# A fourth seven-product quad per gate-and-up column, and half of the other quads' low parts made by an accumulating DMA

## The chip, the cores and the metric

The kernel runs on one core of one Trainium2 chip. The metric is the device time of one execution in microseconds, the median of several runs.

## The reference

A two-layer trunk for 256 tokens of width 2048, all in float32. Both layers end in a SwiGLU block, and this is where the change is:

```python
D_MODEL = 2048; SEQ = 256; D_FF = 5632

def swiglu(h, w_gate, w_up, w_down):
    return (jax.nn.silu(h @ w_gate) * (h @ w_up)) @ w_down

def reference(x, ...):
    for layer in range(2):
        h = rmsnorm(x, g_mix[layer])
        ...
        x = x + mix
        x = x + swiglu(rmsnorm(x, g_ffn[layer]), w_gate[layer], w_up[layer], w_down[layer])
    return rmsnorm(x, g_final)
```

Layer 0 mixes tokens with a gated unit and mean pools, layer 1 with latent attention; both mixers are left as they are.

## The kernel before

**Products in two parts.** TensorE takes float32 operands in a form (float32r, F32R) with fewer bits. So every operand is split: a high part, the value rounded to that form, and a low part, the rest. One product of a 128x128 block of tokens with a 128x512 block of weights is three matmuls (`token_product`, L207 to L209): high x high, high x low, low x high. The weights come as raw tiles of 128x2048 (1 MB, three buffers, issued by SP). ScalarE copies 1024 columns to the high part `wh` (L101), then VectorE subtracts it from the raw tile to give the low part `wl` (L102). There are six tiles of either kind, used in turn, so a new part waits until TensorE is through with the one six parts earlier.

**The feed-forward block** (`feed_forward`, L554). The 5632 hidden columns are worked off in three parts of 4, 4 and 3 columns of 512 (`PARTS`). A column is computed from eight quads j = 0 to 7. A quad is 256 rows of the weights: two row blocks of gate and two of up, four blocks of 128x512 in one raw tile, against 2 x 2 blocks of 128 tokens x 128 features. The four sums c11, c12 (gate and up for the first 128 tokens), c21, c22 stand in PSUM. An eight-quad does the eight block products directly (L579 to L582). A seven-quad does a Strassen-Winograd step with seven (L586 to L594): it needs sums and differences of the four weight blocks, made by VectorE in `quad_seven` (L512), and forms of the tokens' blocks (`forms`, tile `ckv`), made once per layer in `put_pair` (L266). `SEVEN` names the seven-quads, 3, 5 and 7. So a column is 5 x 8 + 3 x 7 = 61 products, 183 matmuls.

The split of a seven-quad is the tile `sums` (t1, t3, t2, t4) and four blocks. In order: VectorE makes t1 and t3 in one subtraction (L519), the first pair of blocks (b22, b21) is split, t2 (L521) and t4 (L522) are made, then the second pair (t2, t4), b11 alone (512 columns) and the third pair (t1, t3) are split. An eight-quad is two splits of 1024 columns.

After a column, ScalarE copies PSUM sums to SBUF, VectorE adds the seven-quads' partial sums in eight additions (L604 to L611), ScalarE applies SiLU and VectorE multiplies; eight transposes on TensorE turn the result, and it is split to `hid`. The transposes wait in a list, `pending`, and are let out after quads 1 and 2 (L595) of the next column. After each part the down projection follows (`into_trunk`), 16 or 12 raw tiles in two plain splits each.

**What sets the order.** `chunks_of` (L532) is a generator of split tiles: it issues loads and splits so that three tiles are ready or under way (`AHEAD` = 2) when one is asked for. The order of instructions on each engine is then set at build time by a scheduler, and each engine works its own queue in order.

Two lines carry most of it:

```python
            nc.scalar.activation(out=wh[:, :m], in_=raw[:, o:o + m], func=AF.Copy)
            nc.vector.tensor_tensor(out=wl[:, :m], in0=raw[:, o:o + m], in1=wh[:, :m].bitcast(F32), op=ALU.subtract)
```

Of the kernel before, what the change touches and what calls it, by code (L numbers as in the profile page):

```python
# [14 lines left out]
P = 128  # L15
# [6 lines left out]

SEVEN = (3, 5, 7)
AHEAD = 2
# [8 lines left out]
def trunk(ctx: ExitStack, tc: tile.TileContext, a: dict, out: bass.AP):  # L33
# [166 lines left out]
    def kept(ps, scale=1.0):  # L200
        r = stat.tile([P, T], F32, name="rstd")
        nc.scalar.activation(out=r, in_=ps, func=AF.Copy, scale=scale)
        return r
# [53 lines left out]
    def into_trunk(w, k0, nk, moving, g, sums, chunks=None, scaled=None):  # L257


        def turn(m, src):  # L260

            def put(pt):
                for j in range(2):
                    split_into(xs[:, m + j, :], pt[:, j * T:(j + 1) * T], gain(g, m + j))

            def put_pair(pt):  # L266
                xg = ev([2, T])
                for j in range(2):
                    nc.scalar.activation(out=xg[:, j, :], in_=pt[:, j * T:(j + 1) * T], func=AF.Copy, scale=gain(g, m + j))
                nc.scalar.activation(out=xs[:, m:m + 2, :T], in_=xg, func=AF.Copy)  # L270
                nc.vector.tensor_tensor(out=xs[:, m:m + 2, T:], in0=xg, in1=xs[:, m:m + 2, :T].bitcast(F32), op=ALU.subtract)
                if m // 2 not in SEVEN:
                    return
                a11, a21, a12, a22 = xg[:, 0, :P], xg[:, 0, P:], xg[:, 1, :P], xg[:, 1, P:]
                f = ev([4, P])
                s1, s2, s3, s4 = (f[:, i, :] for i in range(4))
                nc.vector.tensor_tensor(out=s1, in0=a21, in1=a22, op=ALU.add)
                nc.vector.tensor_tensor(out=s2, in0=s1, in1=a11, op=ALU.subtract)
                nc.vector.tensor_tensor(out=s3, in0=a11, in1=a21, op=ALU.subtract)
                nc.vector.tensor_tensor(out=s4, in0=a12, in1=s2, op=ALU.subtract)  # L280
# [84 lines left out]
    def forms():  # L365

        return big.tile([P, len(SEVEN), 2, 4, P], F32R, name="ckv")

# [55 lines left out]
    with tc.issue_after(gone.ins):  # L424
        nc.scalar.dma_start(out=cnt, in_=a["cnt"])
        nc.scalar.dma_start(out=x, in_=a["xt"])
        nc.scalar.dma_start(out=rope_c, in_=a["rope_c"])
        nc.scalar.dma_start(out=rope_s, in_=a["rope_s"])
    vv = stat.tile([P, 2], F32, name="vv")
# [55 lines left out]
    for m in range(8):  # L485
# [20 lines left out]
        split_into(ab[:, m, :], y)  # L506

    sums, scaled = token_sums(), {"forms": forms()}
    into_trunk(a["w_o0"], 0, KD, ab, "ffn0", sums, scaled=scaled)

# [21 lines left out]
    def chunks_of(layer):  # L532

# [3 lines left out]
        for n in PARTS:  # L537
            for c in range(at, at + n):
                for j in range(KD // 2):
                    todo.append((wgu[c, j], quad_seven if j in SEVEN else quad_eight))  # L540
            for c in range(4):
                for i in range(0, 4 * n, 4):
                    todo.append((wd[c, :, (4 * at + i) * 512:(4 * at + i + 4) * 512], lambda raw: split_raw(raw, 2048)))
            at += n
        ready = []
        for n in range(len(todo)):
            while len(ready) <= AHEAD and todo:
                src, split = todo.pop(0)
                raw = raws.tile([P, 2 * SPLIT], F32, name="raw")
                nc.sync.dma_start(out=raw, in_=src)  # L550
                ready.append(split(raw))
            yield ready.pop(0)

    def feed_forward(layer, sums, scaled, g_next):  # L554
        chunks = chunks_of(layer)
        forms = scaled["forms"]
        f = None
        after = token_sums()
        at = 0
        copy = lambda ps: (e := ev([512]), nc.scalar.activation(out=e, in_=ps, func=AF.Copy))[0]  # L560
        add = lambda out, p, q: nc.vector.tensor_tensor(out=out, in0=p, in1=q, op=ALU.add)  # L561
        for part, n in enumerate(PARTS):
            hid = hidden()
            for c in range(n):
# [8 lines left out]
                for j in range(KD // 2):  # L573
# [4 lines left out]
                    if j not in SEVEN:  # L578
                        for xk, bg, bu in (((x11, x21), "b11", "b12"), ((x12, x22), "b21", "b22")):  # L579
                            for x_t, pg, pu in ((xk[0], c11, c12), (xk[1], c21, c22)):  # L580
                                sum_into(pg, x_t, w[bg], False)
                                sum_into(pu, x_t, w[bu], pu is c22 and xk[0] is x12 and j == max(set(range(KD // 2)) - set(SEVEN)))  # L582
                    else:
                        if j == SEVEN[0]:
                            p1, p6, p5, p7 = (ps_sm.tile([P, 512], F32, name="sm") for _ in range(4))
                        q = forms[:, SEVEN.index(j)]  # L586
                        s1, s2, s3, s4 = ((q[:, 0, i, :], q[:, 1, i, :]) for i in range(4))
                        sum_into(c11, x12, w["b21"], lasting)
# [24 lines left out]
                for t, (g, u) in enumerate(((e11, e12), (e21, e22))):  # L613
                    nc.scalar.activation(out=g, in_=g, func=AF.Silu, scale=f[:, t:t + 1])
                    h = qpool.tile([P, 512], F32, name="qn")
                    nc.vector.scalar_tensor_tensor(out=h, in0=u, scalar=f[:, t:t + 1], in1=g, op0=ALU.mult, op1=ALU.mult)
# [124 lines left out]
    for p in range(10):  # L741
# [4 lines left out]
        for i in range(3):  # L746
# [110 lines left out]
```

## Time and profile before

| | |
|---|---|
| runs | 1936.29 us median of 3 (1935.87 to 1937.83) |
| the profiled execution | 1936.56 us, its span 1934.4 us |
| granted TensorE clock | 0.998 of full speed over the span, that is at the 2.4 GHz level |
| TensorE matmuls | 1920.0 us busy (99%), 9114 |
| VectorE | 1448.0 us (75%), 1793 |
| ScalarE | 1066.6 us (55%), 1426 |
| GpSimd (POOL) | 10.5 us (1%), 27 |
| DMA | 370.94 MB, 192 GB/s over the span |

How to read it: busy time is a share of the whole span, over stages with different limits. The profile names an instruction by the line of the kernel's text, so all splits have the lines L101 and L102, whichever quad they serve. Matmul records overlap (about 390 ns long, one started every 227 ns), so the distance of starts is the price, not the length. A number in brackets behind an instruction is the time for which its engine stood idle before it, with what ended that.

### The profile page before, as it was taken

The page shows a single profiled execution, that of the slowest core. Times are in us where ns is not written, and L with a number is a line of the kernel's source. Part 1 is how long each engine was busy: PE and PEld are TensorE (multiplying, and loading weights), DVE is VectorE, ACT ScalarE, POOL GpSimd, SP SyncE. Part 2 cuts the span into 40 slices and gives each one's busy share as a digit, 9 for nine tenths or more (in the row PEclk, how much of TensorE's full clock was granted, in tenths as well). Part 3 has the DMA queues.
Part 4 walks back from the last instruction along what each step waited for, and adds up shares of the span by engine and source line. Part 5 has one row for each costly group of instructions (what it writes and reads, how often), then busy time and mean ns, then how long its engine had stood idle before and what let it go on. Part 6 is the DMA issues. An engine that isn't in the chain of part 4 may idle for free.

```text
span 1934.4 us, 23510 instructions
## 1 busy us (share of the span) xinstructions
PE 1920.0 (99%) x9114; PEld 1609.2 (83%) x9114; DVE 1448.0 (75%) x1793; ACT 1066.6 (55%) x1426; POOL 10.5 (1%) x27
## 2 busy tenths in 40 slices
PE   9999999999999999999999999999999999999998
PEld 7888888888888888888889988888888888888886
DVE  6685589985688965888675755899956889658984
ACT  6554666563456643555555655665634556435653
POOL 0000000000000000000000000000000000000000
PEclk9999999999999999999999999999999999999999
DMA  8565545565455655556455235455564555654563
GB/s 287 215 217 186 189 175 195 196 218 196 174 196 198 214 197 192 179 196 218 174 194 176 91 131 193 174 197 194 206 208 172 196 198 198 215 196 174 195 239 110
DMA packets 54976, 370.94 MB, mean 192 GB/s; under 512 B 6352, under 2 KB 7888, under 8 KB 10832
## 3 DMA queue, kind: packets, MB, share of 16 engines
q1 hardware_dynamic: 52848, 364.93, 53.8%
q10 hardware_dynamic: 2016, 4.51, 0.7%
q8 instruction: 71, 1.16, 0.2%
q14 instruction: 41, 0.34, 0.0%
HBM read 367.32 MB, written 2.10 MB: 191 GB/s over the span
## 4 chain that ended last, share of the span: by engine, by line
PE 97%; DVE 1%; DMA 1%; ACT 0%; SPq 0%; issue 0%; POOL 0%; ACTq 0%; POOLq 0%
PE mm L207 24%; PE mm L208 24%; PE mm L209 24%; PE mm L131 5%; PE sm L207 3%; PE sm L208 3%; PE sm L209 3%; PE mm L132 2%; PE sm L254 2%; PE mm L402 1%; PE mm L137 1%; PE mm L138 1%; PE mm L136 1%; PE mm L403 1%; PE mm L404 1%; PE sm L705 1%
## 5 line engine op out<-in xcount | busy, mean ns | idle before, releaser
L102 DVE TENSOR_TENSOR wl<-raw,wh 128x1024 fp32r<-128x1024 f32 (+1 forms) x692 | 801.7, 1165 | 339.9 <-ACT wh L101 336.3
L101 ACT ACTIVATE wh<-raw 128x1024 fp32r<-128x1024 f32 (+1 forms) x692 | 694.1, 1013 | 532.6 <-PE mm L209 456.9
L207 PE MATMUL mm<-wh,xs 128*128 128x512 f32 x1012 | 395.3, 391 | 0.0
L209 PE MATMUL mm<-wh,xs 128*128 128x512 f32 x1012 | 393.9, 389 | 0.0
L208 PE MATMUL mm<-wl,xs 128*128 128x512 f32 x1012 | 393.8, 389 | 0.0
L207 PE MATMUL mm<-wh,hid 128*128 128x512 f32 x960 | 375.5, 391 | 0.0
L208 PE MATMUL mm<-wl,hid 128*128 128x512 f32 x960 | 373.7, 389 | 0.0
L209 PE MATMUL mm<-wh,hid 128*128 128x512 f32 x960 | 373.7, 390 | 0.0
L209 PEld LDWEIGHTS mm<-wh,xs 128*128 128x128 f32 x1012 | 190.0, 188 | 39.5
L207 PEld LDWEIGHTS mm<-wh,xs 128*128 128x128 f32 x1012 | 190.0, 188 | 39.0
L208 PEld LDWEIGHTS mm<-wl,xs 128*128 128x128 f32 x1012 | 190.1, 188 | 38.7
L209 PEld LDWEIGHTS mm<-wh,hid 128*128 128x128 f32 x960 | 180.2, 188 | 37.6
L207 PEld LDWEIGHTS mm<-wh,hid 128*128 128x128 f32 x960 | 180.3, 188 | 37.1 <-ACT hid L622 0.3
L208 PEld LDWEIGHTS mm<-wl,hid 128*128 128x128 f32 x960 | 180.3, 188 | 36.5
L102 DVE TENSOR_TENSOR wl<-sums,wh 128x1024 fp32r<-128x1024 f32 x132 | 161.4, 1223 | 63.7 <-ACT wh L101 63.7
L101 ACT ACTIVATE wh<-sums 128x1024 fp32r<-128x1024 f32 x132 | 139.4, 1056 | 126.4 <-DVE sums L516 96.8
L131 PE MATMUL mm<-xs,wh 128*128 128x512 f32 x375 | 133.9, 399 | 0.0
L132 PE MATMUL mm<-xs,wl 128*128 128x256 f32 x375 | 104.8, 280 | 0.0
L131 PEld LDWEIGHTS mm<-xs,wh 128*128 128x128 f32 x375 | 70.4, 188 | 15.9 <-DVE xs L170 0.3
L516 DVE TENSOR_TENSOR sums<-raw 128x1024 f32<-128x1024 f32 x66 | 80.5, 1219 | 0.8 <-DMA raw<-in_w_gu 0.4
L561 DVE TENSOR_TENSOR ev<-sm,ev 128x512 f32<-128x512 f32 x110 | 75.6, 687 | 2.6
L207 PE MATMUL sm<-wh,ckv 128*128 128x512 f32 x198 | 77.0, 389 | 0.0
(205 smaller groups left out, 1914.5 us busy)
## 6 DMA issues: line engine op xcount, KB each, us to landing
raw<-in_w_gu SPq DMA_DIRECT2D x176, 1024.0 KB, 4.8
raw<-in_w_d SPq DMA_DIRECT2D x88, 1024.0 KB, 4.8
raw<-in_w_o SPq DMA_DIRECT2D x32, 1024.0 KB, 4.8
raw<-in_w_v SPq DMA_DIRECT2D x11, 1024.0 KB, 6.2
raw<-in_w_z SPq DMA_DIRECT2D x8, 1024.0 KB, 4.9
raw<-in_w_u SPq DMA_DIRECT2D x8, 1024.0 KB, 4.9
raw<-in_w_q SPq DMA_DIRECT2D x6, 1024.0 KB, 4.8
raw<-in_w_ckv SPq DMA_DIRECT2D x4, 1024.0 KB, 4.8
```

What stands on the lines that cost most here:

```text
L101: nc.scalar.activation(out=wh[:, :m], in_=raw[:, o:o + m], func=AF.Copy)
L102: nc.vector.tensor_tensor(out=wl[:, :m], in0=raw[:, o:o + m], in1=wh[:, :m].bitcast(F32), op=ALU.subtract)
L131: nc.tensor.matmul(ps, lhsT=wh, rhs=mv, start=first, stop=False)
L132: nc.tensor.matmul(ps[:, :T], lhsT=wl, rhs=mv[:, :T], start=False, stop=last)
L136: nc.tensor.matmul(ps[:, :T], lhsT=wh, rhs=mv[:, :T], start=first, stop=False)
L137: nc.tensor.matmul(ps[:, :T], lhsT=wh, rhs=mv[:, T:], start=False, stop=False)
L207: nc.tensor.matmul(ps, lhsT=hi, rhs=wh, start=first, stop=False)
L208: nc.tensor.matmul(ps, lhsT=hi, rhs=wl, start=False, stop=False)
L209: nc.tensor.matmul(ps, lhsT=lo, rhs=wh, start=False, stop=last)
L254: nc.tensor.transpose(pt[:, o:o + P], src(t, j), ident)
L516: sub = lambda out, p, q: nc.vector.tensor_tensor(out=out, in0=p, in1=q, op=ALU.subtract)
L561: add = lambda out, p, q: nc.vector.tensor_tensor(out=out, in0=p, in1=q, op=ALU.add)
```

## The change

1. `SEVEN` becomes (2, 4, 6, 7): four seven-quads per column, four eight-quads (0, 1, 3, 5). The order of quads 0 to 7 stays.
2. In an eight-quad only the first 1024 columns are split as before. For the second 1024 the low part is made otherwise: right after the load, ScalarE writes the negated high part into a tile of its own, `wlx` (pool `low`, two buffers); then POOL issues a DMA that reads the same half of the raw tile from HBM a second time and adds it to `wlx`. The high part goes to `whx` (pool `high`, one buffer).
3. `chunks_of` keeps up to two loads ahead of the split (`loaded`), so that the negated copy and the DMA of a quad come before the split of the quad ahead of it.
4. The form s3 = a11 - a21 is written over a21, and x21's own high and low parts then hold it; three forms per seven-quad are kept instead of four.
5. The transposes of the column before are let out all at once after quad 1 (`SEVEN[0] - 1`).
6. Memory: the pools `att` and `qpool` are opened and closed with their stages; `hds`, `low` and `high` use the same memory in the feed-forward blocks. The two rope tables are loaded when layer 1 begins, not at the start.

```diff
-SEVEN = (3, 5, 7)
+SEVEN = (2, 4, 6, 7)
+EIGHT = tuple(j for j in range(KD // 2) if j not in SEVEN)
...
-    att = pool("att", 1)
-    qpool = pool("qpool", 2)
+    def stage(**bufs):
+
+        st = ExitStack()
+        return st, *(st.enter_context(tc.tile_pool(name=n, bufs=b)) for n, b in bufs.items())
...
-    rope_c = const.tile([P, T], F32, name="rope_c")
-    rope_s = const.tile([P, T], F32, name="rope_s")
...
-                f = ev([4, P])
-                s1, s2, s3, s4 = (f[:, i, :] for i in range(4))
...
-                nc.vector.tensor_tensor(out=s3, in0=a11, in1=a21, op=ALU.subtract)
+                    nc.vector.tensor_tensor(out=a21, in0=a11, in1=a21, op=ALU.subtract)
...
-    def quad_eight(raw):
-        parts = split_raw(raw, 2048)
+    def quad_eight(raw, wl, high):
+
+        parts = split_raw(raw, SPLIT)
+        wh = high.tile([P, SPLIT], F32R, name="whx")
+        nc.scalar.activation(out=wh, in_=raw[:, SPLIT:], func=AF.Copy)
+        parts.append((wh, wl, SPLIT))
         return dict(zip(("b11", "b12", "b22", "b21"), (block(parts, i) for i in range(4))))
...
+        def load(src, kind):
+            raw = raws.tile([P, 2 * SPLIT], F32, name="raw")
+            nc.sync.dma_start(out=raw, in_=src)
+            if kind != "eight":
+                return raw, kind, None
+
+            wl = low.tile([P, SPLIT], F32R, name="wlx")
+            nc.scalar.activation(out=wl, in_=raw[:, SPLIT:], func=AF.Copy, scale=-1.0)
+            nc.gpsimd.dma_start(out=wl, in_=src[:, SPLIT:], accum_op=ALU.add)
+            return raw, kind, wl
+
+        def split(raw, kind, wl):
+            if kind == "plain":
+                return split_raw(raw, 2 * SPLIT)
+            return quad_seven(raw) if kind == "seven" else quad_eight(raw, wl, high)
+
+        loaded, ready = [], []
         for n in range(len(todo)):
-            while len(ready) <= AHEAD and todo:
-                src, split = todo.pop(0)
-                raw = raws.tile([P, 2 * SPLIT], F32, name="raw")
-                nc.sync.dma_start(out=raw, in_=src)
-                ready.append(split(raw))
+            while len(ready) <= AHEAD and (todo or loaded):
+                while todo and len(loaded) < 2:
+                    loaded.append(load(*todo.pop(0)))
+                ready.append(split(*loaded.pop(0)))
             yield ready.pop(0)
...
+        st, hds, low, high = stage(hds=2, low=2, high=1)
+        chunks = chunks_of(layer, low, high)
...
-                        sum_into(p7, s3, w["t3"], lasting)
-                    if j in (1, 2):
-                        next_pending(2)
-                    if j == KD // 2 - 2:
+                        sum_into(p7, x21, w["t3"], lasting)
+                    if j == SEVEN[0] - 1:
+                        next_pending(len(pending))
+                    if j == EIGHT[-1]:
                         e22 = copy(c22)
...
+    st, att, qpool = stage(att=1, qpool=2)
+    rope_c = att.tile([P, T], F32, name="rope_c")
+    rope_s = att.tile([P, T], F32, name="rope_s")
+    nc.scalar.dma_start(out=rope_c, in_=a["rope_c"])
+    nc.scalar.dma_start(out=rope_s, in_=a["rope_s"])
```

**VectorE, the third column of layer 0, before.** Its order of work from quad 4 to the head of quad 6: raw_3045 is the eight-quad 4, raw_3079 the seven-quad 5, raw_3126 the eight-quad 6 (the numbers are the program's).

```order
L102 TENSOR_TENSOR wl_3048<-raw_3045,wh_3047 128x1024
L516 TENSOR_TENSOR sums_3081<-raw_3079 128x1024
L102 TENSOR_TENSOR wl_3052<-raw_3045,wh_3051 128x1024
L102 TENSOR_TENSOR wl_3084<-raw_3079,wh_3083 128x1024
L521 TENSOR_TENSOR sums_3081<-sums_3081,raw_3079 128x512
L516 TENSOR_TENSOR sums_3081<-raw_3079,sums_3081 128x512
L102 TENSOR_TENSOR wl_3090<-sums_3081,wh_3089 128x1024
L102 TENSOR_TENSOR wl_3094<-raw_3079,wh_3093 128x512
L102 TENSOR_TENSOR wl_3098<-sums_3081,wh_3097 128x1024
L102 TENSOR_TENSOR wl_3129<-raw_3126,wh_3128 128x1024
```

**VectorE in the changed kernel, the second column**, quads 6 and 7 (raw_2781 and raw_2813), both seven-quads:

```order
L521 TENSOR_TENSOR sums_2815<-raw_2781 128x1024
L104 TENSOR_TENSOR wl_2818<-raw_2781,wh_2817 128x1024
L526 TENSOR_TENSOR sums_2815<-sums_2815,raw_2781 128x512
L521 TENSOR_TENSOR sums_2815<-raw_2781,sums_2815 128x512
L104 TENSOR_TENSOR wl_2824<-sums_2815,wh_2823 128x1024
L104 TENSOR_TENSOR wl_2828<-raw_2781,wh_2827 128x512
L104 TENSOR_TENSOR wl_2832<-sums_2815,wh_2831 128x1024
L521 TENSOR_TENSOR sums_2861<-raw_2813 128x1024
L104 TENSOR_TENSOR wl_2864<-raw_2813,wh_2863 128x1024
L526 TENSOR_TENSOR sums_2861<-sums_2861,raw_2813 128x512
L521 TENSOR_TENSOR sums_2861<-raw_2813,sums_2861 128x512
L104 TENSOR_TENSOR wl_2870<-sums_2861,wh_2869 128x1024
```

A seven-quad's own seven steps are the same; the low parts of an eight-quad that stood between two of them are gone, and two seven-quads follow each other directly.

**ScalarE at the end of a column, before** (the second one: raw_2857, raw_2893 and raw_2951 are quads 0 to 2 of the next, the third, column; the ev rows on L560 are the copies out of PSUM):

```order
L101 ACTIVATE wh_2832<-sums_2816 128x1024
L101 ACTIVATE wh_2859<-raw_2857 128x1024
L101 ACTIVATE wh_2863<-raw_2857 128x1024
L560 ACTIVATE ev_2891<-mm_2604 128x512
L101 ACTIVATE wh_2895<-raw_2893 128x1024
L560 ACTIVATE ev_2924<-mm_2601 128x512
L101 ACTIVATE wh_2899<-raw_2893 128x1024
L560 ACTIVATE ev_2926<-mm_2602 128x512
L560 ACTIVATE ev_2928<-mm_2603 128x512
L560 ACTIVATE ev_2930<-sm_2756 128x512
L614 ACTIVATE ev_2924<-ev_2924,factor_2571 128x512
L101 ACTIVATE wh_2953<-raw_2951 128x1024
```

**ScalarE in the changed kernel, the same place** (raw_2856, raw_2907, raw_2939 and raw_2995 are quads 0 to 3 of the next column; L562 is the negated copy, L537 whx):

```order
L103 ACTIVATE wh_2877<-sums_2861 128x1024
L562 ACTIVATE wlx_2909<-raw_2907 128x1024
L103 ACTIVATE wh_2912<-raw_2856 128x1024
L103 ACTIVATE wh_2941<-raw_2907 128x1024
L586 ACTIVATE ev_2968<-mm_2632 128x512
L586 ACTIVATE ev_2970<-mm_2633 128x512
L586 ACTIVATE ev_2972<-mm_2634 128x512
L586 ACTIVATE ev_2974<-sm_2757 128x512
L640 ACTIVATE ev_2968<-ev_2968,factor_2602 128x512
L103 ACTIVATE wh_3002<-raw_2939 128x1024
L562 ACTIVATE wlx_2997<-raw_2995 128x1024
L537 ACTIVATE whx_2945<-raw_2907 128x1024
```

The negated copy of quad 1 now stands between the last high part of quad 7 and the first of quad 0, and the negated copy of quad 3 and whx of quad 1 stand behind the first high part of quad 2, ahead of its other three.

## Rows read from the trace of the kernel before

**Rows 1.** The profile page, its parts 1 and 4, whole execution

```profile
PE 1920.0 (99%) x9114; PEld 1609.2 (83%) x9114; DVE 1448.0 (75%) x1793; ACT 1066.6 (55%) x1426; POOL 10.5 (1%) x27
...
PE 97%; DVE 1%; DMA 1%; ACT 0%; SPq 0%; issue 0%; POOL 0%; ACTq 0%; POOLq 0%
```

**Rows 2.** The table by stage: a column, then a down projection; columns in the head

```profile
core 0: us, PE busy (x) PEld busy (x) DVE busy (x) ACT busy (x) POOL busy (x), PEclk, DMA share, GB/s
299.20:341.57 42.37, 42.37 (x194) 35.18 (x192) 38.61 (x44) 25.33 (x31) 0.00 (x0) 1.00 0.58 205
...
426.00:513.00 87.00, 87.00 (x388) 72.14 (x387) 48.41 (x47) 34.61 (x34) 0.00 (x0) 1.00 0.57 200
```

**Rows 3.** The timeline of TensorE in the first column; start us, us, operation

```profile
299.04 1.03 PE L254 MATMUL sm<-ident,qn 128*128 128x128 f32 x8
...
300.61 0.39 PE L207 MATMUL mm<-wh,xs 128*128 128x512 f32 x1
...
305.14 0.39 PE L209 MATMUL mm<-wh,xs 128*128 128x512 f32 x1
...
332.57 0.39 PE L207 MATMUL mm<-wh,xs 128*128 128x512 f32 x1
```

**Rows 4.** The timeline of VectorE, same column; idle before and its releaser in brackets

```profile
300.81 1.28 DVE L623 TENSOR_TENSOR hid<-sm,hid 128x512 fp32r<-128x512 f32 x2
...
306.10 1.22 DVE L516 TENSOR_TENSOR sums<-raw 128x1024 f32<-128x1024 f32 x1
307.23 2.35 DVE L102 TENSOR_TENSOR wl<-raw,wh 128x1024 fp32r<-128x1024 f32 x2
309.50 0.68 DVE L521 TENSOR_TENSOR sums<-sums,raw 128x512 f32<-128x512 f32 x1
310.22 0.69 DVE L516 TENSOR_TENSOR sums<-raw,sums 128x512 f32<-128x512 f32 x1
312.12 1.22 DVE L102 TENSOR_TENSOR wl<-sums,wh 128x1024 fp32r<-128x1024 f32 x1 [1.21 <-ACT wh L101]
313.26 0.68 DVE L102 TENSOR_TENSOR wl<-raw,wh 128x512 fp32r<-128x512 f32 x1
313.87 1.22 DVE L102 TENSOR_TENSOR wl<-sums,wh 128x1024 fp32r<-128x1024 f32 x1
315.00 1.22 DVE L102 TENSOR_TENSOR wl<-raw,wh 128x1024 fp32r<-128x1024 f32 x1
...
334.75 1.28 DVE L561 TENSOR_TENSOR ev<-ev 128x512 f32<-128x512 f32 x2
335.95 0.75 DVE L616 SCALAR_TENSOR_TENSOR qn<-ev,factor 128x512 f32<-128x512 f32 x1
336.61 0.68 DVE L561 TENSOR_TENSOR ev<-sm,ev 128x512 f32<-128x512 f32 x1
```

**Rows 5.** The timeline of ScalarE, same column

```profile
305.63 1.06 ACT L101 ACTIVATE wh<-raw 128x1024 fp32r<-128x1024 f32 x1 [1.16 <-PE mm L209]
...
311.03 1.06 ACT L101 ACTIVATE wh<-sums 128x1024 fp32r<-128x1024 f32 x1 [2.99 <-DVE sums L516]
311.99 0.61 ACT L101 ACTIVATE wh<-raw 128x512 fp32r<-128x512 f32 x1
312.51 1.05 ACT L101 ACTIVATE wh<-sums 128x1024 fp32r<-128x1024 f32 x1
313.47 1.04 ACT L101 ACTIVATE wh<-raw 128x1024 fp32r<-128x1024 f32 x1
```

**Rows 6.** DMA issues (KB, us to landing), SP's waits, the table of one stretch

```profile
raw<-in_w_gu SPq DMA_DIRECT2D x176, 1024.0 KB, 4.8
...
ev<-in_w_s ACTq DMA_DIRECT2D x8, 128.0 KB, 2.2
...
SPq L550 <- DVE wl L102: 1290.3, 260, 9.9
...
62.00:67.00 5.00, 5.00 (x30) 4.41 (x30) 3.31 (x5) 1.62 (x3) 0.19 (x1) 1.00 0.89 371
```

More of the change, by code (lines that the diff above doesn't have):

```diff
@@ L200, in kept @@
     def kept(ps, scale=1.0):
-        r = stat.tile([P, T], F32, name="rstd")
+        r = qpool.tile([P, T], F32, name="rstd")
         nc.scalar.activation(out=r, in_=ps, func=AF.Copy, scale=scale)
@@ L365, in forms @@
     def forms():
-        return big.tile([P, len(SEVEN), 2, 4, P], F32R, name="ckv")
+        return big.tile([P, len(SEVEN), 2, 3, P], F32R, name="ckv")
     gfin = None
@@ L506, in trunk @@
         split_into(ab[:, m, :], y)
+    st.close()
     sums, scaled = token_sums(), {"forms": forms()}
@@ L526, in quad_seven, with chunks_of @@
         return dict(zip(("b22", "b21", "t2", "t4", "b11", "", "t1", "t3"), (block(parts, i) for i in range(8))))
-    def quad_eight(raw):
-        parts = split_raw(raw, 2048)
+    def quad_eight(raw, wl, high):
[3 more added lines that the diff above has]
+        parts.append((wh, wl, SPLIT))
         return dict(zip(("b11", "b12", "b22", "b21"), (block(parts, i) for i in range(4))))
-    def chunks_of(layer):
+    def chunks_of(layer, low, high):
         wgu, wd = a[f"w_gu{layer}"], a[f"w_d{layer}"]
@@ L539, in chunks_of @@
                 for j in range(KD // 2):
-                    todo.append((wgu[c, j], quad_seven if j in SEVEN else quad_eight))
+                    todo.append((wgu[c, j], "seven" if j in SEVEN else "eight"))
             for c in range(4):
                 for i in range(0, 4 * n, 4):
-                    todo.append((wd[c, :, (4 * at + i) * 512:(4 * at + i + 4) * 512], lambda raw: split_raw(raw, 2048)))
+                    todo.append((wd[c, :, (4 * at + i) * 512:(4 * at + i + 4) * 512], "plain"))
             at += n
-        ready = []
-        for n in range(len(todo)):
-            while len(ready) <= AHEAD and todo:
-                src, split = todo.pop(0)
-                raw = raws.tile([P, 2 * SPLIT], F32, name="raw")
-                nc.sync.dma_start(out=raw, in_=src)
-                ready.append(split(raw))
+        def load(src, kind):
[12 more added lines that the diff above has]
+        loaded, ready = [], []
+        for n in range(len(todo)):
+            while len(ready) <= AHEAD and (todo or loaded):
+                while todo and len(loaded) < 2:
+                    loaded.append(load(*todo.pop(0)))
+                ready.append(split(*loaded.pop(0)))
             yield ready.pop(0)
     def feed_forward(layer, sums, scaled, g_next):
-        chunks = chunks_of(layer)
         forms = scaled["forms"]
@@ L581, in feed_forward @@
                                 sum_into(pg, x_t, w[bg], False)
-                                sum_into(pu, x_t, w[bu], pu is c22 and xk[0] is x12 and j == max(set(range(KD // 2)) - set(SEVEN)))
+                                sum_into(pu, x_t, w[bu], pu is c22 and xk[0] is x12 and j == EIGHT[-1])
                     else:
@@ L586, in feed_forward @@
                         q = forms[:, SEVEN.index(j)]
-                        s1, s2, s3, s4 = ((q[:, 0, i, :], q[:, 1, i, :]) for i in range(4))
+                        s1, s2, s4 = ((q[:, 0, i, :], q[:, 1, i, :]) for i in range(3))
                         sum_into(c11, x12, w["b21"], lasting)
@@ L614, in feed_forward @@
                     nc.scalar.activation(out=g, in_=g, func=AF.Silu, scale=f[:, t:t + 1])
-                    h = qpool.tile([P, 512], F32, name="qn")
+                    h = hds.tile([P, 512], F32, name="hd")
                     nc.vector.scalar_tensor_tensor(out=h, in0=u, scalar=f[:, t:t + 1], in1=g, op0=ALU.mult, op1=ALU.mult)
@@ L631, in feed_forward @@
             at += n
+        st.close()
         return after
@@ L648, in trunk @@
     ckv = big.tile([P, 4, 2 * T], F32R, name="ckv")
+    st, att, qpool = stage(att=1, qpool=2)
+    rope_c = att.tile([P, T], F32, name="rope_c")
+    rope_s = att.tile([P, T], F32, name="rope_s")
+    nc.scalar.dma_start(out=rope_c, in_=a["rope_c"])
+    nc.scalar.dma_start(out=rope_s, in_=a["rope_s"])
     kz = att.tile([P, 2, T], F32, name="dd")
```

17 lines of the change are left out of this document (10 added, 7 removed).

## The prediction

> **What bounds the kernel now.** I read the page first: TensorE is busy for 1920.0 us of the 1934.4 us span, and 97% of the chain that ended last is its own matmuls [rows 1]. So a removed matmul is worth its full time only as long as nothing else takes over the pace. The table by stage shows where that is near: in a gate-and-up column TensorE works 42.37 of 42.37 us and VectorE 38.61, in the down projection VectorE only 48.41 of 87 [rows 2]. The timeline of TensorE gives the price of a matmul: from 300.61 to 332.57 us lie 47 products of three, 0.680 us each [rows 3]; 61 products are 41.48 us, the rest of the column is eight transposes. The timeline of VectorE shows how its work hangs on ScalarE [rows 4]: in a seven-quad the second block's high part can be made only when t4 is there, so from t4's start at 310.22 to the next low part at 312.12 lie 1.90 us, of which 1.21 are an empty wait. Two such waits stand in a column now; 38.61 busy us and 2.42 of waits are 41.03, less than the 42.37 of TensorE. That margin of 1.3 us is what the change spends.
>
> **The sum, part by part.**
> *TensorE.* 22 columns lose one product each, 22 x 0.68 = 15.0 us; a column of 61 products becomes 60, 41.69 us with its transposes. If nothing else changed, the profiled execution's 1936.56 us would be 1921.6.
>
> *VectorE.* The order above shows its row of work for a seven-quad: subtraction, first low part, t2, t4, second low part, third, fourth. From the starts in [rows 4] the steps are 1.13 (306.10 to 307.23), 1.14, 0.72 (309.50 to 310.22), 1.90 with the wait, 1.14, 0.61 and 1.13: 7.77 us. Nothing stands between t4 and the second low part for quads 4, 6 and 7, so three full ones are 23.3. Quad 2 is mixed with the column's eight additions and two products with SiLU: its own work is 1.13 + 1.14 + 2 x 0.60 + 1.14 + 0.61 + 1.13 = 6.35 and a wait of 1.90 - 0.60 - 0.67 = 0.6 is left. Additions 8 x 0.60 (two in 1.20, from 334.75 to 335.95), products 2 x 0.66 (335.95 to 336.61), the two splits of the hidden tile 1.28. The four eight-quads have one low part each, 4 x 1.14 = 4.6. One wait more: on ScalarE the next column's first high part now stands behind the fourth high part of quad 7 and a negated copy, so it starts 0.96 + 0.52 + 0.96 + 0.96 = 3.40 us after quad 7's second high part and frees VectorE 1.09 later [rows 5], at 4.49, when VectorE would be ready at 1.09 + 1.14 + 0.61 + 1.13 = 3.97: 0.5 us. Sum: 23.3 + 6.35 + 0.6 + 4.8 + 1.3 + 1.3 + 4.6 + 0.5 = 42.7 us. So from the second column of a part on, VectorE and ScalarE need **42.7 us where TensorE needs 41.69**: 1.0 us short per column, although the ten low parts of five eight-quads have become four.
>
> *The lead.* A part does not lose this at once. In its later columns the single tile whx makes ScalarE wait for TensorE at the end of quad 0: 24 x 0.2267 = 5.44, and 0.26 until ScalarE starts (305.37 to 305.63) [rows 3, 5]. Behind this wait stand a negated copy and whx (0.96 each), then quad 2's second high part (1.09): its low part begins at 8.71 and ends the quad at 11.59; quads 3, 4, 5, 6 add 1.14 + 7.77 + 1.14 + 7.77, quad 7 to the end of its second low part 1.13 + 1.14 + 0.72 + 1.90 + 1.22 = 6.11: 35.5. TensorE, without transposes in a first column, wants that block at 4 x 5.44 + 3 x 4.76 + 1.36 + 0.23 = 37.6. So a part starts with about 2.1 us in hand. With a deficit d per column, a part of four columns loses 3d - 2.1 and a part of three 2d - 2.1: over both layers 16d - 12.6.
>
> *ScalarE.* It was busy 25.3 us in a column [rows 2]; a seven-quad has three copies of 1024 and one of 512, an eight-quad two, from now on three (the negated one is new), so 3 x 3 + 5 x 2 = 19 long ones become 4 x 3 + 4 x 3 = 24: 5 x 0.96 + 0.52 = 5.3 us more [rows 5], 31 of 42, no bound by itself. But its order matters, as above. Its queue now also waits for loads: behind the negated copy of quad 3 stand whx of quad 1, the second SiLU and quad 2's remaining high parts, and TensorE wants whx in the middle of quad 1, at 5.44 + 2.72 = 8.16; ScalarE has it at 5.70 + 0.96 + 1.06 = 7.7. Half a microsecond.
>
> *The accumulating DMAs.* 88 of 512 KB. TensorE wants them late: quad 3's copy is made about 6 us into the column and used at 19.5, so 13 us are there, and a load of 1024 KB lands in 4.8 [rows 6]. I cost the wait for them at nothing. What they disturb is another matter. The trace has no accumulating transfer, so its price is bounded by rows of plain ones: 128 KB land in 2.2 us, 1024 KB in 4.8, thus 2.6 us for 896 KB and 1.5 for 512 KB. The one for quad 1 is issued about 0.5 us after the load of quad 2: both hang on quad 7 (load: its third low part, 1.09 + 1.14 + 0.68 + 0.1 = 3.0 us after the second high part; accumulate: the negated copy, 2.44 + 1.06 + 0.1 = 3.6). VectorE wants quad 2 at 8.0 (3.97 + 0.5 + 2 x 1.14 + 2 x 0.6), and the load lands at 3.0 + 4.8 = 7.8: **0.2 us to spare**. SP can't issue it sooner, it waits for VectorE's low parts as all its loads do [rows 6]. If the two transfers share the engines, the load is late by the other's work: 1.5 us at the rate of one load, 1.0 at the 371 / 0.89 = 417 GB/s of the stretch in which two queues were full [rows 6]. Less the 0.2: 0.8 to 1.3 us per column. Below, nothing at all, if the accumulate starts only when the load has landed; above, twice 1.5, if an accumulate must read its destination too, 2.8. I take the plain transfer, since its rows are of the same tensors and shape, and the middle, 1.05.
> The Trainium skill (DMA: Bandwidth & Descriptors, section "Issuing engines are not separate DMA queues") says that DMAs of all issuing engines run on the same 16 engines and interleave. That rule speaks against this change: by it the delay stands, and with separate engines it would be 0 and the time that of the first rival.
>
> *Costed at nothing.* A fourth set of forms, small VectorE operations once per layer, beside TensorE's first column; the two rope loads, which ScalarE now issues during the last down projection of layer 0; the shared pool memory, whose old users end before that projection. SP issues the same loads in the same order. If ScalarE had to wait for the rope loads there, it would be 2.2 us each [rows 6], once, and the cover is the down projection, where VectorE is busy for 48 of 87 us [rows 2].
>
> **Sum.** d = 1.0 + 1.05 = 2.1: 16 x 2.1 - 12.6 = 21.0 us lost, 15.0 won: 1936.56 + 6.0 = 1942.6 for a profiled execution. That one stands 0.3 us over the median shown, 1936.29, so I say **1942 us**. About 0.2%, 3.9 us, is what a measurement of this kernel can tell from no change; the forecast is slower by 0.3%.
>
> **Rivals.**
> 1. *The accumulate does not meet the load* (d = 1.0). Only the last column of a four-column part stalls: 4 x (3.0 - 2.1) = 3.6 us, so 1936.3 - 15.0 + 3.6 = 1925. For it: the issue by POOL may start its data later than SP's does, and nothing in the trace shows when. Against it: the load takes 3 us on the engines, a late accumulate still meets its end. It decides at d = 1.7, a delay of 0.7: below that the change wins. Chance 0.22.
> 2. *TensorE still sets the pace*, VectorE's waits are filled: 1921 us. For it: the waits in VectorE's sum are those of one column, and a column now begins at other distances from TensorE. Against: the order leaves nothing between t4 and the low part. 0.12.
> 3. *An accumulate costs twice a copy*: a delay of 1.8 to 2.8, d = 2.8 to 3.8, 32 to 48 us lost, 1954 to 1969. For it: it must add to what lies there. Against: no row. 0.24.
> 4. *POOL can issue only in VectorE's gaps.* VectorE is 91% busy and waits once per seven-quad, and these begin up to 4.76 + 5.44 = 10.2 us apart; with 2.2 + 2.6 x 384 / 896 = 3.3 us to land that is 13.5 against the 13 there are: 0.5 us on each of 22 columns beside the forecast's loss, 1953. 0.04. The Trainium skill (SBUF — State Buffer, section "SBUF: two separate sides") tells of such a starvation when VectorE runs a mode that takes both ports; no row of POOL here shows a DMA issue.
> The forecast itself has 0.31, the rest (0.07) is spread over both sides.
>
> **How the numbers follow.** Faster by over 0.2% (under 1932.4): rival 1 but for its upper edge, rival 2 and a little of the rest: 0.36. Within 0.2%: the forecast's lower edge (0.8 us of delay gives 1938) and rival 1's upper: 0.16. Slower: 0.48. The range of 8 in 10 reaches from rival 2's 1921 edge, taken at 1922, to 1966 in rival 3. The forecast alone would be 1938 to 1946.
>
> **What would show it.** Right: TensorE's first columns of a part at 41.7 us, the third and fourth at 43 to 44, with TensorE waiting for VectorE's low parts in quad 7 and 2; VectorE waiting for the load before quad 2's subtraction; raw loads landing in 5.5 us or more beside an accumulate. Wrong: all columns at 41.7 (rival 2); loads at 4.8 us and stalls only in fourth columns (rival 1); accumulates landing after 6 us and every column over 44 (rival 3); TensorE waiting for the accumulate itself (rival 4).

## The result, and the profile after

The changed kernel takes 2000.99 us (median of 4 runs, 2000.0 to 2002.44) beside 1936.08 us for the kernel before on the same chip: a ratio of 1.0342, 95% interval 1.0329 to 1.0354. It is slower by 65 us, where I forecast 6 us and gave 1966 as the upper end.

The page's busy times and its row on the chain, which answer to [rows 1]:

```profile
PE 1932.0 (97%) x9048; PEld 1604.9 (80%) x9048; DVE 1438.3 (72%) x1825; ACT 1174.7 (59%) x1560; POOL 87.0 (4%) x115
...
PE 62%; DMA 14%; DVE 13%; ACT 6%; issue 4%; POOL 0%; SPq 0%; ACTq 0%; POOLq 0%; DVEq 0%
```

The matmuls are fewer by 66, the 22 products, yet TensorE is busy 12 us longer, and its matmuls are only 62% of the chain (97% before); loads have 14% of it and VectorE 13%. The view of TensorE's waits (us in total, times, longest) names who keeps it:

```profile
PE mm L209 <- ACT whx L537: 36.6, 13, 5.2
PE sm L209 <- ACT ev L271: 5.8, 2, 3.3
PE mm L210 <- DVE wl L104: 5.4, 9, 0.8
```

The largest is the wait for `whx`, the high part of an eight-quad's second half. The table by stage, for the four columns of one part (columns as in [rows 2]), shows in which columns the time goes:

```profile
514.40:555.20 40.80, 40.80 (x181) 33.74 (x180) 25.75 (x28) 24.70 (x28) 3.46 (x4) 1.00 0.72 205
555.20:602.90 47.70, 43.63 (x189) 35.70 (x189) 39.18 (x45) 31.03 (x39) 3.46 (x4) 0.96 0.72 229
602.90:646.30 43.40, 42.54 (x189) 34.38 (x188) 37.11 (x45) 29.29 (x36) 3.46 (x4) 1.00 0.77 235
646.30:692.30 46.00, 43.41 (x189) 35.58 (x189) 39.79 (x47) 29.76 (x37) 1.73 (x2) 0.96 0.72 225
```

The first column takes 40.80 us, which is 180 matmuls of 0.2267: there the product is won in full. The others take 47.7, 43.4 and 46.0 us where 41.69 would be TensorE's own. In the second and fourth the granted clock is 0.96. How the second column loses 6 us is seen in its first 13 us. ScalarE (timeline, with the idle time before a row and its releaser):

```profile
550.65 1.05 ACT L537 ACTIVATE whx<-raw 128x1024 fp32r<-128x1024 f32 x1
...
559.25 1.06 ACT L103 ACTIVATE wh<-raw 128x1024 fp32r<-128x1024 f32 x1 [3.26 <-DMA raw<-in_w_gu]
560.22 0.58 ACT L586 ACTIVATE ev<-sm 128x512 f32<-128x512 f32 x1
560.70 0.71 ACT L640 ACTIVATE ev<-ev,factor 128x512 f32<-128x512 f32 x1
564.12 1.06 ACT L103 ACTIVATE wh<-sums 128x1024 fp32r<-128x1024 f32 x1 [2.71 <-DVE sums L521]
565.08 0.61 ACT L103 ACTIVATE wh<-raw 128x512 fp32r<-128x512 f32 x1
565.60 1.04 ACT L103 ACTIVATE wh<-sums 128x1024 fp32r<-128x1024 f32 x1
566.55 1.04 ACT L537 ACTIVATE whx<-raw 128x1024 fp32r<-128x1024 f32 x1
```

The issues of POOL and SP (same timeline):

```profile
550.52 0.86 POOL L563 DMA_DIRECT2D wlx<-in_w_gu  x1 [4.43 <-ACT wlx L562]
551.50 3.89 SPq L557 DMA_DIRECT2D raw<-in_w_gu  x2
```

And TensorE:

```profile
563.19 0.39 PE L211 MATMUL mm<-wh,xs 128*128 128x512 f32 x1
567.64 0.50 PE L209 MATMUL mm<-whx,xs 128*128 128x512 f32 x1 [4.07 <-ACT whx L537]
567.98 0.52 PE L210 MATMUL mm<-wlx,xs 128*128 128x512 f32 x1
568.30 0.63 PE L211 MATMUL mm<-whx,xs 128*128 128x512 f32 x1
568.72 0.63 PE L209 MATMUL mm<-whx,xs 128*128 128x512 f32 x1
```

Read backwards: TensorE stands 4.07 us for whx of quad 1. ScalarE makes it at 566.55, behind all of quad 2's high parts; those wait 2.71 us for VectorE's t4 and, before that, 3.26 us for quad 2's raw tile. Its load was issued at 551.50 and releases ScalarE at 559.25, 7.7 us where [rows 6] have 4.8; POOL had issued the accumulating DMA of quad 1 at 550.52.

When TensorE resumes, its matmuls start 0.43 us apart instead of 0.227, and the granted clock of this stretch is 0.56 of full speed, so mostly at its lower level of 1.2 GHz (table by stage):

```profile
567.60:571.50 3.90, 3.86 (x10) 3.04 (x11) 3.90 (x6) 2.50 (x3) 0.86 (x1) 0.56 0.68 252
```

Over the span the granted clock is 0.989, 0.998 before; 0.9% of 2000.7 us, 18 us, is my estimate of what the slower stretches cost.

The order shown ahead of the prediction, with whx of quad 1 ahead of quad 2's other three high parts and behind quad 3's negated copy, is that of other columns. The one that it was read from starts at 333.87 (rows of ScalarE, of SP and POOL, and of TensorE):

```profile
336.89 1.06 ACT L103 ACTIVATE wh<-raw 128x1024 fp32r<-128x1024 f32 x1 [0.53 <-DMA raw<-in_w_gu]
344.19 1.06 ACT L562 ACTIVATE wlx<-raw 128x1024 fp32r<-128x1024 f32 x1 [6.23 <-DMA raw<-in_w_gu]
345.15 1.04 ACT L537 ACTIVATE whx<-raw 128x1024 fp32r<-128x1024 f32 x1
...
331.14 3.09 SPq L557 DMA_DIRECT2D raw<-in_w_gu  x2
331.96 0.86 POOL L563 DMA_DIRECT2D wlx<-in_w_gu  x1 [6.18 <-ACT wlx L562]
...
346.24 0.80 PE L209 MATMUL mm<-whx,xs 128*128 128x512 f32 x1 [4.03 <-ACT whx L537]
```

Here quad 2's tile holds ScalarE up by only 0.53 us, but quad 3's negated copy waits 6.23 us: quad 3's load, the second of the two issues, at 333.90, lands 10.2 us later, and whx stands behind that copy. Of the 13 waits for whx, six are of this second kind (17.1 us), four of the first (17.9 us); the other three, 1.6 us, stand behind a SiLU that waits for VectorE.

The page's rows on queues (packets, MB, share of 16 engines) and on issues (KB, median us to landing):

```profile
q1 hardware_dynamic: 52848, 364.93, 50.3%
q0 software_dynamic: 12672, 46.14, 13.7%
...
raw<-in_w_gu SPq DMA_DIRECT2D x176, 1024.0 KB, 7.0
raw<-in_w_d SPq DMA_DIRECT2D x88, 1024.0 KB, 4.8
...
wlx<-in_w_gu POOLq DMA_DIRECT2D x88, 512.0 KB, 7.4
```

The gate-and-up loads now land in 7.0 us, those of the down projection, which have no accumulates beside them, in 4.8 as before.

### The profile page after: what moved, and what is told of

Read it like the earlier page. It is cut to its first block, busy times and chain, and to the rows that moved or that the text cites. A ratio compares the mean times of both kernels' runs of the same rounds, so it can differ in the third digit from the quotient of the medians.

```text
span 2000.7 us, 23763 instructions
## 1 busy us (share of the span) xinstructions
PE 1932.0 (97%) x9048; PEld 1604.9 (80%) x9048; DVE 1438.3 (72%) x1825; ACT 1174.7 (59%) x1560; POOL 87.0 (4%) x115
## 3 DMA queue, kind: packets, MB, share of 16 engines
q0 software_dynamic: 12672, 46.14, 13.7%
## 4 chain that ended last, share of the span: by engine, by line
PE 62%; DMA 14%; DVE 13%; ACT 6%; issue 4%; POOL 0%; SPq 0%; ACTq 0%; POOLq 0%; DVEq 0%
PE mm L209 15%; PE mm L210 15%; PE mm L211 15%; DMA raw<-in_w_gu 13%; DVE wl L104 6%; PE mm L133 4%; ACT wh L103 4%; DVE sums L521 2%; PE mm L134 2%; PE sm L209 2%; PE sm L211 2%; PE sm L210 2%; DVE ev L587 1%; ACT whx L537 1%; DVE sums L526 1%
## 5 line engine op out<-in xcount | busy, mean ns | idle before, releaser
L104 DVE TENSOR_TENSOR wl<-raw,wh 128x1024 fp32r<-128x1024 f32 (+1 forms) x604 | 682.5, 1136 | 286.2 <-ACT wh L103 284.9
L103 ACT ACTIVATE wh<-raw 128x1024 fp32r<-128x1024 f32 (+1 forms) x604 | 588.5, 985 | 389.9 <-PE mm L211 272.3
L210 PE MATMUL mm<-wl,xs 128*128 128x512 f32 x528 | 207.3, 393 | 5.4 <-DVE wl L104 5.4
L209 PE MATMUL mm<-wh,xs 128*128 128x512 f32 x528 | 208.5, 395 | 1.5 <-ACT wh L103 0.8
L211 PE MATMUL mm<-wh,xs 128*128 128x512 f32 x528 | 206.2, 391 | 0.0
L209 PE MATMUL mm<-whx,xs 128*128 128x512 f32 x352 | 144.5, 411 | 36.6 <-ACT whx L537 36.6
L562 ACT ACTIVATE wlx<-raw 128x1024 fp32r<-128x1024 f32 x88 | 92.9, 1056 | 125.1 <-DMA raw<-in_w_gu 114.1
L210 PE MATMUL mm<-wlx,xs 128*128 128x512 f32 x352 | 141.7, 403 | 0.0
L211 PE MATMUL mm<-whx,xs 128*128 128x512 f32 x352 | 141.7, 402 | 0.0
L521 DVE TENSOR_TENSOR sums<-raw 128x1024 f32<-128x1024 f32 x88 | 107.6, 1222 | 45.6 <-DMA raw<-in_w_gu 44.8
L563 POOL DMA_DIRECT2D wlx<-in_w_gu x88 | 76.4, 869 | 1232.6 <-ACT wlx L562 1024.6
L210 PEld LDWEIGHTS mm<-wl,xs 128*128 128x128 f32 x528 | 99.6, 189 | 28.8 <-DVE wl L104 8.6
L209 PEld LDWEIGHTS mm<-wh,xs 128*128 128x128 f32 x528 | 99.5, 188 | 24.0 <-ACT wh L103 2.6
```

The source lines that it names most:

```text
L209: nc.tensor.matmul(ps, lhsT=hi, rhs=wh, start=first, stop=False)
L210: nc.tensor.matmul(ps, lhsT=hi, rhs=wl, start=False, stop=False)
L211: nc.tensor.matmul(ps, lhsT=lo, rhs=wh, start=False, stop=last)
L521: sub = lambda out, p, q: nc.vector.tensor_tensor(out=out, in0=p, in1=q, op=ALU.subtract)
L562: nc.scalar.activation(out=wl, in_=raw[:, SPLIT:], func=AF.Copy, scale=-1.0)
L563: nc.gpsimd.dma_start(out=wl, in_=src[:, SPLIT:], accum_op=ALU.add)
```

## The experiments

Behind each time stands, in brackets, its ratio to the kernel before, measured beside it (1933.8 to 1934.7 us), and the 95% interval of that ratio.

**The size of the transfer.** Two kernels keep every engine's instructions in the order of the changed kernel and alter the DMA alone.

```diff
-            nc.gpsimd.dma_start(out=wl, in_=src[:, SPLIT:], accum_op=ALU.add)
+            nc.gpsimd.dma_start(out=wl[:, :64], in_=src[:, SPLIT:SPLIT + 64], accum_op=ALU.add)
```

```diff
-            nc.gpsimd.dma_start(out=wl, in_=src[:, SPLIT:], accum_op=ALU.add)
+            nc.gpsimd.dma_start(out=wl, in_=src[:, SPLIT:])
```

> The change with each accumulating DMA cut to the first 64 of its 1024 columns (32 KB for 512), so the low parts of these blocks are incomplete; every engine keeps its instructions in the same order. Theory A (the accumulates' time on the DMA engines makes the raw load of quad 2 late, 7.7 us for 4.8, and whx of quad 1 waits behind that load's copies in ScalarE's queue): raw loads of the gate-up weights land in 4.7 to 5.3 us, TensorE's waits for whx fall from 36.6 to under 6 us, the clock's falls during gate-and-up go, and the time is 1930 to 1945. Rival B (order and buffers alone: negated copies, one whx, three raw tiles): the whx waits stay above 25 us and the time above 1980. Rival C (the prediction's rate of VectorE, 42.7 us a column): about 1925, with waits for low parts in each fourth column.

> The change with a plain DMA of the same 512 KB in place of the accumulating one, so the tile holds the raw weights and no low part; same instructions in the same order. If an accumulate costs twice a copy (queue 0 has 13.7% of 16 engines for 46 MB, 3.1 us of all engines per transfer, where 1.45 is half a raw load), queue 0 falls to about 7%, raw loads land in 5.3 to 6.2 us, and theory A gives 1940 to 1970. If the size of the transfer alone counts, the time stays at 1995 to 2005. Rival B: 1980 or more as well.

The first took 1928.48 us (0.9971, 0.9958 to 0.9985), 1.5 us under the range of theory A, the second 1959.08 (1.0121, 1.0092 to 1.015), inside it. The waits for whx are gone in the first and 15.4 us in the second. ScalarE's own waits for gate-and-up loads, at negated copies and high parts, are 158.9 us in the change (114.1 and 44.8) and 44.6 in the first run (41.5 and 3.1). Their queue and issue rows, first run, then second:

```profile
q0 software_dynamic: 12672, 2.89, 1.7%
...
raw<-in_w_gu SPq DMA_DIRECT2D x176, 1024.0 KB, 4.9
```

```profile
q0 software_dynamic: 12672, 46.14, 7.7%
...
raw<-in_w_gu SPq DMA_DIRECT2D x176, 1024.0 KB, 5.9
```

So the time follows the transfer, 2001, 1959 and 1928.5 us for loads of 7.0, 5.9 and 4.9: theory A holds and rival B, order and buffers alone, falls. The price of an accumulate also comes out. 13.7% of 16 engines over 2000.7 us, for 88 transfers, is 3.1 us of all engines each; the plain copy, 7.7% of 1957.3 us, is 1.7. An accumulate costs 1.8 copies. The columns of the first run show what VectorE needs when loads land in 4.9 us (second to fourth column of a part):

```profile
542.40:584.10 41.70, 41.70 (x189) 34.62 (x188) 37.51 (x45) 29.94 (x38) 3.45 (x4) 1.00 0.58 198
584.10:625.80 41.70, 41.70 (x189) 34.62 (x188) 37.11 (x44) 29.66 (x37) 3.45 (x4) 1.00 0.56 197
625.80:667.50 41.70, 41.70 (x189) 34.62 (x188) 37.45 (x44) 27.41 (x33) 1.73 (x2) 1.00 0.55 196
```

TensorE sets the pace in all of them, so rival C falls: my rate of 42.7 us is too high. VectorE's busy 37.5 us and its waits (1.23, 1.21, 1.13 and 0.40 in the first of these columns) are 41.5: it keeps up with 0.2 us to spare.

**Which accumulate.** One run cuts only quad 1's DMA to 64 columns (the kind "eight" is quad 1 here); the other run has the two sizes exchanged and cuts the three others.

```diff
...
+            m = 64 if kind == "eight" else SPLIT
+            nc.gpsimd.dma_start(out=wl[:, :m], in_=src[:, SPLIT:SPLIT + m], accum_op=ALU.add)
```

> The change with the accumulating DMA of quad 1 alone cut to its first 64 columns (so that block's low part is incomplete); the other three of a column are full, every engine keeps its order. Theory A1 (it is quad 1's accumulate, issued 1 us ahead of quad 2's load, that makes this load late): the waits for whx fall from 36.6 to under 12 us, and the time is 1930 to 1960. If the four accumulates of a column have equal shares of the 72 us between the change and the run with all four cut: 1983, with waits for whx above 20 us.

> The counterpart: quad 1's accumulate is full, those of quads 0, 3 and 5 are cut to 64 columns. Theory A1: waits for whx stay above 25 us and the time is 1970 to 2001. Equal shares: 1946.

Measured: 1968.11 us (1.0172, 1.0145 to 1.02) and 1956.37 (1.0111, 1.0091 to 1.0132). Both times miss what theory A1 said, and both miss equal shares. Over the 1928.5 us of the run with all four cut, quad 1's alone costs 28 us and the other three together 40, about 13 each; the two add up to 68 of the 72.5. The waits for whx are 7.8 us in the first and 21.1 in the second. So quad 1's accumulate is behind most of the waits for whx, and costs more than the average of the others, but the others cost time too; they were not cut one by one. The reading that followed, which the next runs try: with 0.2 us to spare, VectorE passes on each late load.

**The place of whx, and VectorE's reserve.** A second whx tile (with six ev tiles for seven, for the memory) lets the scheduler put whx of quad 1 ahead of quad 2's copies:

```diff
-    evs = pool("evs", 7)
+    evs = pool("evs", 6)
...
-        st, hds, low, high = stage(hds=2, low=2, high=1)
+        st, hds, low, high = stage(hds=2, low=2, high=2)
```

> The change with two whx tiles for one (and six ev tiles for seven, to make room). In ScalarE's order whx of quad 1 then stands ahead of quad 2's copies, behind those of quad 0 and 1. Theory A with the place in the queue as its second half: waits of TensorE for whx fall under 8 us, raw loads stay at 6.5 to 7.5 us, and quad 2's late low parts show 2 to 3 us later as waits of TensorE for VectorE's wl; 1950 to 1975. If the place does not count (the load is late anyway and everything hangs on it): 1990 or more.

The other edit splits (t2, t4) last in a seven-quad, with its two products last too; VectorE then works on b11 and (t1, t3) while ScalarE makes the high part of (t2, t4):

```diff
-        parts += split_raw(sums[:, 1024:], 1024)
         parts += split_raw(raw[:, :512], 512)
         parts += split_raw(sums[:, :1024], 1024)
+        parts += split_raw(sums[:, 1024:], 1024)
...
```

> The change with all four accumulating DMAs and one whx, but in each seven-quad (t2, t4) split last. After eight runs two causes stand: (1) whx of quad 1 stands in ScalarE's queue behind copies that wait for a late load, with the clock's falls behind it; (2) VectorE has only 0.2 to 0.6 us to spare in a column (37.5 busy and 3.6 of waits for ScalarE of 41.69), so that a late load anywhere goes through to TensorE. This edit gives VectorE some 3.6 us per column and so takes (2) away alone; in ScalarE's order whx of quad 1 now stands behind all copies of quad 2 and one of quad 3. Expected: waits of TensorE for whx stay above 30 us, waits for VectorE's low parts fall under 3 us (8 now), 1965 to 2010. If VectorE's shortage were the whole of it: 1920 to 1935.

> The same with two whx tiles (and six ev tiles for seven): both causes taken away, all four accumulates kept, raw loads still late (6 to 7 us). If the two causes are all, 1921 to 1935 against 1957 for two whx tiles alone; if the late loads cost TensorE in a third way, 1940 or more.

| | one whx | two whx |
|---|---|---|
| (t2, t4) second | 2001.0 (the change) | 1957.0 (1.011, 1.0081 to 1.014) |
| (t2, t4) last | 1960.4 (1.0133, 1.0112 to 1.0154) | 1926.1 (0.9953, 0.9936 to 0.9969) |

Either edit is worth over 40 us, and both 75, as much as cutting the transfers (72.5), though the transfers are all there. The queue and issue rows of the kernel with both:

```profile
q0 software_dynamic: 12672, 46.14, 13.3%
...
raw<-in_w_gu SPq DMA_DIRECT2D x176, 1024.0 KB, 6.8
```

Its loads land in 6.8 us, and TensorE's waits come to 9.7 us in all, 59.5 in the change.

Two of the expectations failed in part. With two whx tiles and the old order no wait for whx is left, as expected, but loads landed in 6.0 us, and quad 2's low parts cost TensorE only 1.5 us; its largest waits are for VectorE's products with SiLU (6.7 us) and the low parts of the hidden tile (6.1), so for VectorE elsewhere. With (t2, t4) last and one whx I had over 30 us of waits for whx and at least 1965 us, since whx stands behind even more copies there. There are no such waits, but the cost has only moved. TensorE now waits for ScalarE's copies out of PSUM, and ScalarE for the one whx tile:

```profile
PE mm L209 <- ACT ev L586: 10.7, 9, 2.4
ACT whx L537 <- PE mm L211: 53.8, 41, 2.9
```

In one such column these copies stand behind a high part of quad 2 that waits 1.94 us for its load. The second tile is still worth 34 us with the new order (1960.4 against 1926.1). I read this as a late load that costs through whatever stands behind its copies on ScalarE. No run parts the second tile from the six ev tiles that came with it.

**VectorE's shortage with little transfer.** There is one accumulate per column, quad 5's; the other eight-quads are split on VectorE. The first run has the old order of splits, the second (t2, t4) last.

```diff
-                    todo.append((wgu[c, j], "seven" if j in SEVEN else "eight"))
+                    todo.append((wgu[c, j], "seven" if j in SEVEN else "eight" if j in (5,) else "plain8"))
...
+            if kind == "plain8":
+                return dict(zip(("b11", "b12", "b22", "b21"), (block(p, i) for p in [split_raw(raw, 2 * SPLIT)] for i in range(4))))
```

> One accumulating DMA per column, at quad 5, with the old order of splits in a seven-quad: no transfer beside quad 2's load. Cause (2) alone: VectorE needs 37.3 + 3 x 1.14 + 3.6 of waits = 44.3 us a column, 2.6 us more than TensorE, so about 16 x 2.6 - 12.6 = 29 us of the 15 won are lost: 1940 to 1960, with waits for low parts. If the transfers alone cost: 1920 to 1928, like the run with (t2, t4) last.

> The same with one accumulating DMA per column, that of quad 5, whose transfer falls between the loads of quads 6 and 7 and not beside that of quad 2. VectorE 40.8 us per column. 1921 to 1930 if this accumulate disturbs nothing; if a load beside an accumulate is late wherever it is, loads of 7 us and waits of TensorE or VectorE about quad 7, 1935 to 1960.

Old order: 1972.83 us (1.0197, 1.0177 to 1.0218). Loads land in 4.8 us, and from quad 5 to quad 5 of the next column the later columns still take 44.8 and 45.7 us:

```profile
581.20:626.00 44.80, 44.01 (x190) 34.01 (x189) 40.60 (x46) 27.40 (x34) 0.88 (x1) 1.00 0.56 191
626.00:671.70 45.70, 43.72 (x190) 34.09 (x189) 41.38 (x48) 27.44 (x34) 0.88 (x1) 1.00 0.58 198
```

VectorE is busy 40.6 and 41.4 us; I read the rest as its waits. The shortage is then the one worked out, 44.3, or up to 1.4 more, and the time is 13 us over what I expected. With (t2, t4) last: **1920.94 us (0.9927, 0.991 to 0.9943)**, faster than both kernels.

```profile
542.70:584.40 41.70, 41.70 (x189) 34.59 (x189) 40.99 (x48) 28.29 (x35) 0.88 (x1) 1.00 0.63 216
584.40:626.10 41.70, 41.70 (x190) 34.56 (x189) 41.01 (x48) 28.30 (x35) 0.88 (x1) 1.00 0.63 213
```

VectorE is busy 41.0 of 41.70 us, and the wait of 1.21 us in [rows 4] is gone. Its timeline in quad 6 of this kernel:

```profile
569.81 0.69 DVE L521 TENSOR_TENSOR sums<-raw,sums 128x512 f32<-128x512 f32 x1
570.41 2.52 DVE L104 TENSOR_TENSOR wl<-sums,wh 128x1024 fp32r<-128x1024 f32 x2
572.85 1.22 DVE L104 TENSOR_TENSOR wl<-raw,wh 128x1024 fp32r<-128x1024 f32 x1
```

After t4 at 569.81 the next low part starts 0.60 later, not 1.90.

**No accumulate at all**, (t2, t4) last:

> Four seven-quads without any accumulating DMA: eight-quads are split on VectorE as in the kernel before, and in a seven-quad the pair (t2, t4) is split last (its products come last too), so that VectorE works on b11 and (t1, t3) while ScalarE makes the high part of (t2, t4). VectorE: 37.3 busy us of the run with cut accumulates plus 4 x 1.14 = 41.9 per column, without the 1.2 us waits; TensorE 41.69. If these waits are all that kept VectorE from it, the time is 1922 to 1932, faster than the kernel before by 0.2 to 0.6%. If VectorE waits for ScalarE elsewhere (over 1 us per column), 1935 to 1950.

This took 1926.82 us (0.996, 0.9945 to 0.9975), inside the range, with all four seven-quads and no extra transfer; VectorE is busy 40.3 to 41.4 us of 41.70.

**Two controls.** `SEVEN = (3, 5, 7)` with the accumulating DMAs, and the same without them but with (t2, t4) last:

> The change with SEVEN = (3, 5, 7): 61 products per column as before, five eight-quads with accumulating DMAs (110 in all), VectorE five low parts lighter per column than before. If VectorE's shortage from the fourth seven-quad is what costs, the time is 1936 within 5 us. If the accumulates are (theory A), raw loads land in 6 us or more, TensorE waits for whx by over 15 us in all, and the time is 1950 to 2000.

> Control: three seven-quads (3, 5, 7) as in the kernel before, no accumulating DMA, but all the rest of the change (pools shared by stages, s3 over a21, rope tables at layer 1, two loads ahead, transposes all at once) and (t2, t4) split last. If the gain of the runs with one or no accumulate comes from the seventh product of a fourth quad alone, and the rest is free as the prediction had it, the time is that of the kernel before within 4 us: 1930 to 1938. If the late split or the rest is worth something by itself, 1920 to 1928, and those runs owe less to the product; if the rest costs, over 1940.

The first took 2057.47 us (1.0629, 1.0599 to 1.066), worse than the change though VectorE has less to do, and 57 us above what I expected. Loads land in 7.0 us, and here TensorE waits for the accumulate itself:

```profile
PE mm L210 <- DMA wlx<-in_w_gu: 29.4, 20, 3.3
PE mm L209 <- ACT whx L537: 26.5, 16, 3.5
PE mm L209 <- DVE x L307: 19.6, 8, 3.9
```

So the transfers cost much even where VectorE has less to do. Whether five accumulates a column are too many for two wlx tiles, and what stands behind the third row, was not tried. The second took 1934.11 us (0.9996, 0.9987 to 1.0006): with three seven-quads the pools, the forms, the rope tables, the look-ahead and the late split are together worth nothing, and what the faster kernels win is the product. With the fourth seven-quad the late split is what lets them win it (1972.8 against 1920.9 above).

## Why the prediction was wrong

*TensorE, 15.0 us:* right. The first columns of parts, which have no transposes, take 40.80 us where I had put 41.7, the later ones 41.7 in the run with cut accumulates, and the best version wins 13.0 us, 1933.94 - 1920.94.

*VectorE's sum, 42.7 us per column:* too high by 1.2. The run with cut accumulates has 41.5. I had quad 2's wait at 0.6; the eight additions fill it whole. Most of the rest is that its busy steps add up to 37.5 us, not 38.0. But it was no reason for ease: 0.2 us of reserve is next to none.

That "slower" came true was in part luck. The late load was real, but of my d = 1.0 + 1.05 the 1.0 does not exist, and with 1.05 alone my formula loses 4.2 us against 15.0 won: 1925, faster.

*The accumulate's price, "I take the plain transfer":* the first step that failed. It costs 1.8 copies, 3.1 us of all engines. "Above, twice 1.5" was the right end of the range, and rival 3 (0.24) had this price; its 1954 to 1969 still lie below 2001. (The lower bound of the plain one was also off: 512 KB at 417 GB/s are 1.26 us, not 1.0, which would have made the forecast 1944.) The Trainium skill (DMA: Bandwidth & Descriptors, section "Rules for kernel authors") says that an accumulate reads its destination and writes it later. The measured 3.1 against 1.7 us agrees with that; no row here shows the read itself.

*"The one for quad 1 is issued about 0.5 us after the load of quad 2", and no other meeting:* I let only this accumulate delay only this load. It is 28 of the 72.5 us, the other three are 40, and the late load that holds whx up is quad 3's in six of the 13 waits. Loads go from 4.8 to 7.0 us, so rival 1 (0.22) is gone. The Trainium skill (DMA: Bandwidth & Descriptors, section "Issuing engines are not separate DMA queues"), which I weighed against the change, has the DMAs of all engines interleave on the same 16 engines. The 7.0 us beside accumulates, 5.9 beside plain transfers and 4.9 beside cut ones agree with it.

*ScalarE, "TensorE wants whx at 8.16; ScalarE has it at 7.7. Half a microsecond":* the step that mattered most. The 7.7 is a row of copies that starts at 5.70 with quad 3's negated copy, and so takes quad 3's load as landed, though I had said that the queue now waits for loads. In the column from 333.87 this copy starts at 344.19, 10.3 us into the column and not 5.7: the 4.6 us more, less the half in hand, are about the wait of 4.03. I had also read the order in one column and taken it for all; in the columns of the first kind whx stands behind all of quad 2's copies, and so waits for quad 2's load and for t4. These are the 36.6 us of waits, and the 18 us of clock behind them, which I had not counted at all.

*The lead, 16d - 12.6:* the formula is for a slow rate, smoothed over a part. A stop in the second column, as in the one from 555.20, isn't smoothed. My reading is that the lead is in VectorE's low parts, while TensorE lacks one copy on ScalarE. I forecast 43 to 44 us for the third and fourth columns; 47.7 in the second is the sign that it was a stop and not the rate.

*Costed at nothing:* the first columns of the layers wait 5.8 us for the token forms (L271), which stand behind a late negated copy; with cut accumulates that is 0.3. The pools, rope tables and the order of transposes were rightly nothing. Of rival 4 the rows show no sign: POOL issued quad 1's accumulate, at 550.52, 0.3 us after the end of its negated copy.

The span's 66.3 us more and the 15.0 won make 81 us of losses. TensorE's waits in the view shown above come to 59.5 us in all, 5.4 in the kernel before, so 54 more: 36.6 for whx, 5.8 for the forms, 5.4 for low parts, the others small. With the estimated 18 for the clock that is 72. The rest, some 9 us, I have not taken apart.

## What to carry to other kernels

Late loads cost what the engines behind them cannot catch up: the same transfers left 1926 us where VectorE's waits were filled and whx stood early, and 2001 where neither held. Before an engine's work is given to a DMA, look for the empty waits in that engine's own order: moving one pair of splits made so much room that VectorE could do the low parts of three accumulates, or all four, itself. And price a late load at every instruction that stands behind its copies in an in-order queue, not only at its own consumer.

## What I had not expected of the hardware

An accumulating DMA of 512 KB took 3.1 us of all 16 engines, a plain one from the same queue 1.7, and one of 32 KB 0.4 (1.7% of 1926.7 us, 88 transfers). A stop of TensorE of 4 us was followed by matmuls 0.43 us apart for a few microseconds, at a granted clock of 0.56; over the span, as estimated above, such stretches cost about 18 us beside the 36.6 of the waits for whx. And a load of 1 MB that landed in 4.8 us in the kernel before took 10.2 from its issue, behind another load and beside an accumulate.
